# A two-layer trunk on one Trainium2 core: sixteen more weight tiles split into pairs ahead of their use, h put into PSUM by ScalarE for the output projection, and more time for two kinds of transfers

## The chip, the core and the metric

The kernel runs on one core of a Trainium2 chip. The core has a matmul engine (TensorE, PE in the profile, with its weight loads as PEld), three engines for everything else (VectorE, DVE; ScalarE, ACT; GpSimd, POOL), and a synchronising engine (SyncE, SP) that here issues nearly all transfers between the chip's memory and on-chip memory (SBUF), over 16 DMA engines. Matmuls write into PSUM, in eight banks of 128 x 512 float32. The engines run side by side and wait for each other by semaphores; each takes its own instructions in the order in which they stand. The metric is the device time of one execution, in microseconds, as the median of several runs.

## The reference

The reference is a decoder trunk on one sequence of 1024 tokens with 1024 features, in two layers, all in float32. Layer 0 mixes tokens with a gated MLP over chunks of 128 tokens, layer 1 with dilated windowed attention in three groups of heads, whose outputs are merged by their softmax weights. After each mixer comes a dense MLP of width 4096 with a squared ReLU:

```
x = x + mixer_i(rms_norm(x, g))                      i = 0: gating, 1: attention
x = x + relu(rms_norm(x, g') @ w_up[i]) ** 2 @ w_down[i]
...
out = rms_norm(x, g_final)

# attention, per dilation group: unnormalised sums, then merged
m_all = max over groups of m_;   c = exp(m_ - m_all)
o = sum(num * c) / sum(den * c);   x = x + o @ w_out
```

## The kernel before

Activations are kept transposed, features on partitions: `h[m]` is features 128m to 128m+127 by 1024 tokens, worked on in two halves of 512 tokens. A float32 operand is **split** into a pair: ScalarE writes a rounded high part (L213) and VectorE the remainder (L214). One product of two pairs is three matmuls, `three` at L326: high by high, high by low, low by high. All matmuls are issued at L185; six of them of 128 x 512 take about 1.36 us when TensorE does not wait.

The program runs through these stages (us from the start of the profiled execution): gating mixer to 305; first MLP, up to 623 and down to 910, closing to 936; values and attention to 1448; output projection to 1520; second MLP, up to 1823 and down to 2123; final norm to 2162.

**MLP.** The hidden width is worked on in 16 steps q. The first two are done plainly for the two halves of tokens; from q = 2 on, each step is a scheme of seven products (a, d, e and so on in `mlp`) of sums of weight tiles with sums of activations, 84 matmuls, about 19 us a step. `Weights` (L337) loads four raw tiles of a step, forms their sums on GpSimd and splits the seven results one by one, one at each call of `more`; each result goes into a slot that a product of the step before has freed. In layer 0, from q = 5 on, the second, fourth and sixth call of `more` also advance `prepare_late`, a side line that loads a weight tile of a later stage, splits it and stores the pair in memory (`wl`), where `late` fetches it ready for use. Before, it does this for eight tiles of the second MLP's first steps and eight of the output projection. The down phase (`Down`) does likewise seven products at a time over groups of up to four steps, adding into `h` in SBUF by VectorE (L962). The sums that several products share are kept in `u` (L981). Its last part, `close`, multiplies the hidden tiles of q = 15 (`xe`) by plain weights (`we`).

**Attention.** Twelve units of heads go through scores, softmax, transposes (`turned`) and values. The seven products of each unit's q, k weights come from `prepare`, which loads four raw tiles of a unit, waits a given time (`own is raw`: 8000 ns), then forms sums on VectorE (L487, L488 and on), splits them and stores them in memory (`wd`). `exchange` sends the softmax sums of a unit through memory into the order of another group; `merge` combines three groups, with 12000 ns (`LAT["ex"]`) planned for the exchange. `split_N` makes a merged output a pair, `outs[hp, i]` for head pair hp and token half i.

**Output projection.** `project(i, hps)` runs over the eight column blocks m; for each it sums the products of the head pairs `hps` in a bank and VectorE adds the bank to `h[m]` (L313). First the head pairs 0 to 2 of half 0, then of half 1 as filling between the last attention unit's work, then the last head pair of each half, after which the half's norm and y for the second MLP are made (`start_terms`).

**Order of the work.** TensorE's instructions stand in the order in which the program issues them (`manual_schedule` for TensorE). While it issues, `Flow` keeps a planned clock of TensorE's time, to which each matmul adds its length, and side lines (`flow.add`) whose steps are put in when the planned clock has reached their due time (`yield` of a time, or of an event and a time after it). `flow.until` moves the planned clock on until something is there. So the times in `LAT`, the `yield`s and the delay given to `flow.add` decide between which matmuls a side line's matmuls stand; nothing makes the real engines keep to them. The other engines' order comes from a scheduler. `bias_rows` (L1039) is such a side line: three times it loads a table, waits 12000 ns, casts it on ScalarE (L1045), multiplies it by the bias table and stores the row.

## Time and profile before

| | |
|---|---|
| median of 3 runs | 2161.12 us (2159.89 to 2166.99) |
| the profiled execution, its own time | 2163.61 us |
| its span in the trace | 2161.9 us |
| mean granted TensorE clock | 0.992 |
| matmul records | 10192 |
| DMA traffic | 367.68 MB, 170 GB/s on average |

The page gives busy time, share of the span and count for each engine. A group of instructions is named by line, engine, operation and tiles (`out<-in`, buffer numbers left out). Behind a row of the timeline stands in brackets how long the engine was idle before it, and what ended that. The numbers behind the engines in a row of windows are the granted TensorE clock, the share of the 16 DMA engines in use, and GB/s. TensorE's instructions are all L185 (matmuls) or L192 (transposes), so places in the program are told by tiles and time: `y` is a normalised input, `wp` a weight pair, `mm` and `at` are banks, `r` and `t` raw tiles and temporaries, `V` a unit's values, `o` a merged output.

### The profile page before, as it was taken

What the parts mean: (1) busy time and instruction counts of PE and PEld (TensorE: products, weight loads), DVE (VectorE), ACT (ScalarE), POOL (GpSimd) and SP (SyncE); (2) the same over time, 40 slices, a digit from 0 to 9 for tenths busy, and PEclk for the clock granted to TensorE, in tenths of its full rate; (3) what the DMA queues carried; (4) which work ended last, traced back from release to release, by engine and by line L of the source; (5) the groups of instructions that cost most, each with busy time, mean ns of one, the idle gap of its engine ahead of it and who ended that gap; (6) DMA issues with size and microseconds to landing.
All of it is one profiled execution on the core that took longest, in us unless ns stands there. A gap on an engine that the chain in (4) does not pass through costs nothing.

```text
span 2161.9 us, 30552 instructions
## 1 busy us (share of the span) xinstructions
PE 2119.5 (98%) x10192; PEld 1747.0 (81%) x10192; DVE 1560.9 (72%) x2897; ACT 1143.8 (53%) x2308; POOL 510.7 (24%) x381
## 2 busy tenths in 40 slices
PE   8999998999999999999999999999999999999997
PEld 7888887888888888878877788777788888888886
DVE  7877678655689787798357666758885555988776
ACT  7645445555565444355266665645455556544442
POOL 2000224323323333420200000001433322333344
PEclk9999999999999999999999999999999999999999
DMA  6326713566655443359787646491254443654432
GB/s 215 124 81 217 274 57 133 180 213 219 217 167 194 155 160 118 103 183 335 269 280 228 178 153 180 158 268 40 84 190 152 157 159 115 207 169 145 149 99 78
DMA packets 214962, 367.68 MB, mean 170 GB/s; under 512 B 38809, under 2 KB 66580, under 8 KB 214804
## 3 DMA queue, kind: packets, MB, share of 16 engines
q1 hardware_dynamic: 205664, 364.37, 50.5%
q10 hardware_dynamic: 9140, 1.36, 0.4%
q8 instruction: 80, 1.31, 0.2%
q14 instruction: 78, 0.64, 0.1%
HBM read 239.13 MB, written 126.52 MB: 169 GB/s over the span
## 4 chain that ended last, share of the span: by engine, by line
PE 81%; DVE 8%; DMA 4%; ACT 3%; issue 2%; SPq 0%; POOL 0%; DVEq 0%; POOLq 0%; ACTq 0%
PE at L185 42%; PE mm L185 39%; PE at L192 1%; DMA wp<-wd 1%; DVE h L313 1%; DVE hx L214 1%; DVE t L1486 1%; DVE tr L214 1%; DVE y L214 1%; DMA h<-in_xT 0%; DVE wp L214 0%; ACT t L1319 0%; DVE N L1358 0%; DMA r<-in_w_v 0%; DVE r L415 0%
## 5 line engine op out<-in xcount | busy, mean ns | idle before, releaser
L213 ACT ACTIVATE wp<-r 128x512 fp32r<-128x512 f32 (+2 forms) x411 | 243.8, 598 | 360.7 <-PE at L185 276.7
L214 DVE TENSOR_TENSOR wp<-r,wp 128x512 fp32r<-128x512 f32 (+2 forms) x404 | 323.7, 806 | 129.7 <-ACT wp L213 126.1
L185 PE MATMUL at<-hx,wp 128*128 128x512 f32 x1740 | 405.7, 389 | 1.4 <-DVE h L962 1.4
L185 PEld LDWEIGHTS at<-hx,wp 128*128 128x128 f32 x1740 | 326.5, 188 | 70.0 <-DVE h L962 2.2
L185 PE MATMUL mm<-t,wp 128*128 128x512 f32 x1368 | 345.5, 396 | 1.0 <-DVE k L1243 1.0
L185 PEld LDWEIGHTS mm<-t,wp 128*128 128x128 f32 x1368 | 251.2, 188 | 55.0 <-DVE k L1243 2.1
L269 POOL TENSOR_TENSOR t<-t 128x512 f32<-128x512 f32 (+1 forms) x64 | 81.9, 1281 | 714.6 <-ACT t L264 558.3
L185 PE MATMUL at<-y,wp 128*128 128x512 f32 x1008 | 246.5, 391 | 0.0
L185 PEld LDWEIGHTS at<-y,wp 128*128 128x128 f32 x1008 | 189.9, 189 | 40.2 <-issue 0.7
L185 PE MATMUL mm<-y,wp 128*128 128x512 f32 x816 | 216.5, 405 | 1.9 <-issue 1.2
L356 POOL TENSOR_TENSOR t<-r 128x512 f32<-128x512 f32 (+3 forms) x62 | 80.1, 1291 | 470.0 <-DMA r<-in_w_up 148.8
L185 PEld LDWEIGHTS mm<-y,wp 128*128 128x128 f32 x816 | 152.5, 193 | 35.2 <-issue 2.2
L185 PE MATMUL mm<-hx,wp 128*128 128x512 f32 x696 | 169.1, 389 | 0.0
L214 DVE TENSOR_TENSOR hx<-t,hx 128x512 fp32r<-128x512 f32 x192 | 156.7, 820 | 3.2 <-ACT hx L213 2.9
L185 PE MATMUL mm<-y,whi 128*128 128x512 f32 x512 | 158.1, 390 | 0.0
L185 PEld LDWEIGHTS mm<-hx,wp 128*128 128x128 f32 x696 | 130.4, 188 | 27.9 <-DVE b L981 0.9
L358 POOL TENSOR_TENSOR r<-r 128x512 f32<-128x512 f32 (+3 forms) x62 | 90.9, 1466 | 181.4 <-DVE wp L214 162.5
L213 ACT ACTIVATE hx<-t 128x512 fp32r<-128x512 f32 x192 | 119.6, 630 | 25.4 <-DMA t<-hid 20.0
L185 PE MATMUL at<-t,wp 128*128 128x512 f32 x552 | 130.6, 389 | 0.0
L962 DVE TENSOR_TENSOR h<-h,at 128x512 f32<-128x512 f32 x144 | 98.0, 681 | 42.6 <-PE at L185 42.0
L185 PEld LDWEIGHTS at<-t,wp 128*128 128x128 f32 x552 | 103.6, 188 | 21.5
L185 PEld LDWEIGHTS mm<-y,whi 128*128 128x128 f32 x512 | 95.6, 188 | 19.5
(225 smaller groups left out, 3452.8 us busy)
## 6 DMA issues: line engine op xcount, KB each, us to landing
t<-hid SPq DMA_DIRECT2D x182, 256.0 KB, 4.0
wd<-tr SPq DMA_DIRECT2D x154, 256.0 KB, 3.3
wp<-wd SPq DMA_DIRECT2D x77, 512.0 KB, 5.3
hid<-t SPq DMA_DIRECT2D x140, 256.0 KB, 2.9
r<-in_w_up SPq DMA_DIRECT2D x120, 256.0 KB, 2.7
r<-in_w_dn SPq DMA_DIRECT2D x80, 256.0 KB, 2.6
hid<-b SPq DMA_DIRECT2D x56, 256.0 KB, 2.9
r<-in_w_v SPq DMA_DIRECT2D x48, 256.0 KB, 3.7
```

The lines of the kernel that those rows point to most:

```text
L185: nc.tensor.matmul(out, lhsT, rhs, **kw)
L192: nc.tensor.transpose(out, src, ident)
L213: nc.scalar.activation(hi, src, AF.Copy)
L214: (engine or nc.vector).tensor_tensor(lo, src, hi.bitcast(F32), op=ALU.subtract)
L269: nc.gpsimd.tensor_tensor(self.acc, self.acc, sq, op=ALU.add)
L313: nc.vector.tensor_tensor(x, x, ps, op=ALU.add)
L356: tt(r3, r[0, 0], r[1, 0], op=ALU.subtract)
L358: tt(r[1, 1], r[1, 0], r[0, 0], op=ALU.subtract)
L962: return engine.tensor_tensor(hs[i, s], hs[i, s], src, op=ALU.add).ins
L1486: nc.vector.tensor_tensor(own(t, g), permuted(us_[g].N, i, g), own(pb, g), op=ALU.mult)
```

## The change

- `LATE` has 16 more tiles: the closing weights of both MLPs (`dl`) and the first set of value weights (`vt`). They are no longer split where they are used but loaded as pairs with `late`. The side line now does one tile at each of its turns: it loads the next tile and splits the one before, in place (the remainder is written over the raw tile). The two stores of a tile are issued at the next turn (`save`). So the steps q = 5 to 15 of layer 0 take three tiles each where they took one and a half. Each added tile costs two more stores of 256 KB in memory traffic and a load of 512 KB in place of one of 256 KB.
- In the down phase, from t = 4 on, the shared sum stays in PSUM: ScalarE copies the bank to a second bank (`sums`), and the product with w[6] is accumulated there, where VectorE added the bank to `u` before. 28 such adds of VectorE become 28 copies of ScalarE.
- In `project` for head pairs 0 to 2, ScalarE copies h into the bank before the products and the bank back into h after them. Only the column blocks 0 to 5 are done so; blocks 6 and 7 of each half are done at the end with all four head pairs in one bank, and added by VectorE.
- Planned times: the bias rows begin 120000 ns later, with 6000 ns between cast and matmul; raw weights get 18000 instead of 8000 ns; the exchange 15000 instead of 12000 ns, and a merge waits for both exchanges and 3000 ns.

`Weights` also gets a parameter for its order, whose default is the order as it was.

```diff
 OPEN = 5
+WHOLE = 6
+FIRST = 6
 LATER = (2, 4, 6)
 ...
 PACE = (2100.0, 2500.0, 1900.0, 3500.0)
-LAT = dict(sum=2600.0, rms=2600.0, tile=1600.0, gate=8500.0, soft=5500.0, turn=4200.0, fe=1300.0, v=2000.0, qk=4200.0, merge=2600.0, out=700.0, fex=3.0, ve=1600.0, vd=6000.0, ex=12000.0)
+LAT = dict(sum=2600.0, rms=2600.0, tile=1600.0, gate=8500.0, soft=5500.0, turn=4200.0, fe=1300.0, v=2000.0, qk=4200.0, merge=2600.0, out=700.0, fex=3.0, ve=1600.0, vd=6000.0, ex=15000.0)
 ...
             r00, r10, r01, r11 = (load(w_qkv[n + a][:, half(b)], own()) for a, b in ((0, 0), (1, 0), (0, 1), (1, 1)))
-            yield max(pace, 8000.0) if own is raw else pace
+            yield max(pace, 18000.0) if own is raw else pace
 ...
-    LATE = {("up", q, i, j): (w_up[1, q, i, j]) for q in range(2) for j in range(2) for i in range(2)}
+    LATE = {("dl", 0, a): w_dl[0, a] for a in range(4)}
+    LATE.update({("up", q, i, j): (w_up[1, q, i, j]) for q in range(2) for j in range(2) for i in range(2)})
     LATE.update({("bo", hp, b): w_bo[hp][:, half(b)] for hp in range(4) for b in range(2)})
+    LATE.update({("vt", k): w_vt[0, k] for k in range(KT)})
+    LATE.update({("dl", 1, a): w_dl[1, a] for a in range(4)})
     wl = {key: dram.tile([P, 2, HALF], F32, name="wl" + "_".join(map(str, key)), bufs=1) for key in LATE}
 ...
+    def fetch(src):
+        r = rtemp()
+        return r, load(src, r.bitcast(F32))
+
+    unsaved = []
+
+    def save():
+        for dst, t in unsaved:
+            nc.sync.dma_start(dst, t.bitcast(F32))
+        unsaved.clear()
+
+    def placed(dst, held):
+        lo, r = held
+        hi = rtemp()
+        split(hi, lo, r)
+        unsaved.extend((dst[:, e, :], t) for e, t in enumerate((hi, lo)))
+
 ...
-        for key, src in LATE.items():
-            r = load(src, temp())
+        keys = list(LATE)
+        held = fetch(LATE[keys[0]])
+        yield
+        for n, key in enumerate(keys):
+            last, held = held, fetch(LATE[keys[n + 1]]) if n + 1 < len(keys) else None
+            placed(wl[key], last)
             yield
-            hi, lo = rtemp(), rtemp()
-            split(hi, lo, r)
-            for e, t in enumerate((hi, lo)):
-                nc.sync.dma_start(wl[key][:, e, :], t.bitcast(F32))
-            yield
 ...
-    def late(*key):
-        t = wpool.tile([P, 2, HALF], F32R, tag="w", name="wp")
-        nc.sync.dma_start(t.bitcast(F32), wl[key])
-        return Pair(t)
+    def late(*key, place=None):
+        w = (place or wpair)()
+        nc.sync.dma_start(w.t.bitcast(F32), wl[key])
+        return w
 ...
                 if layer == 0 and q >= OPEN and calls[0] in LATER:
+                    save()
                     next(coming_late, None)
+                if layer == 0 and q == 15 and calls[0] == 7:
+                    save()
 ...
                     more()
-                    nc.vector.tensor_tensor(self.u[a], self.u[a], a_, op=ALU.add)
+                    sums = mm_bank()
+                    nc.scalar.activation(sums, a_, AF.Copy)
                     self.inputs(t + 1, (1,))
 ...
                     self.ends(1)
-                b = at_bank()
-                product(b, w[6], xs(6))
+                b = at_bank() if t < 4 else sums
+                product(b, w[6], xs(6), t >= 4)
                 then(nc.vector.tensor_tensor(self.u[a], self.u[a], b, op=ALU.add).ins, 6)
 ...
                 self.xe = {}
-                self.we = [pair("we").split(load(w_dl[self.layer, a], temp())) for a in range(4)]
+                self.we = [late("dl", self.layer, a, place=lambda: pair("we")) for a in range(4)]
             for j in range(2):
 ...
             nc.scalar.activation(oh[0:33, 0:VEC], raw[0:33, 0:VEC], AF.Copy)
+            yield 6000
             ps = at_bank()
 ...
     def value_weights(r, place=None):
+        if r == 0:
+            return [late("vt", k) for k in range(KT)]
         return [(place or wpair)().split(load(w_vt[r, k])) for k in range(KT)]
 ...
-    flow.add(bias_rows())
+    flow.add(bias_rows(), 120000.0)
     firsts = []
 ...
     ex = {}
+    exchanged = {(hp, g): Event() for hp in range(4) for g in (1, 2)}
 ...
         ex[u.hp, g] = e
+        exchanged[u.hp, g].t = flow.t
 ...
+        for g in (1, 2):
+            yield exchanged[hp, g], 3000
         us_ = {u.g: u for u in U if u.hp == hp}
 ...
-    def project(i, hps, after=None):
-        for m in range(KT):
-            b = mm_bank()
+    def project(i, hps, after=None, ms=range(KT)):
+        held, ms = {}, list(ms)
+
+        def begin(m):
+            held[m] = mm_bank()
+            if not after:
+                nc.scalar.activation(held[m], h[m][:, half(i)], AF.Copy)
+
+        begin(ms[0])
+        for n, m in enumerate(ms):
+            b = held.pop(m)
             for hp in hps:
-                three(b, wbo[hp, m // 4], blk(m % 4), outs[hp, i], hp == hps[0], hp == hps[-1])
+                three(b, wbo[hp, m // 4], blk(m % 4), outs[hp, i], bool(after) and hp == hps[0], hp == hps[-1],
+                      skip_group_check=True)
+                if hp == hps[0] and n + 1 < len(ms):
+                    begin(ms[n + 1])
                 flow.pump()
-            add_h(m, half(i), b)
             if after:
+                add_h(m, half(i), b)
                 after(m)
+            else:
+                nc.scalar.activation(h[m][:, half(i)], b, AF.Copy)
             yield
 ...
     flow.pump()
-    for _ in project(0, range(3)):
+    for _ in project(0, range(3), ms=range(FIRST)):
         pass
 ...
     outs_load(2, 1)
-    rest = project(1, range(3))
+    rest = project(1, range(3), ms=range(WHOLE))
     while (3, 0) not in outs and next(rest, 1) is None:
 ...
         proj_load(3, b)
-    for _ in project(0, [3], sq[0].add):
+    for _ in project(0, [3], sq[0].add, range(FIRST)):
         pass
+    if FIRST < KT:
+        for _ in project(0, range(4), sq[0].add, range(FIRST, KT)):
+            pass
     start_terms(sq[0], 0, 3, terms)
 ...
     flow.until(lambda: (3, 1) in outs)
-    for _ in project(1, [3], sq[1].add):
+    for _ in project(1, [3], sq[1].add, range(WHOLE)):
         pass
+    if WHOLE < KT:
+        for _ in project(1, range(4), sq[1].add, range(WHOLE, KT)):
+            pass
     start_terms(sq[1], 1, 3, terms)
 ...
         first[q][i, j] = late("up", q, i, j)
```

Three places of the new order matter for the steps of the prediction. Lines of the changed program are 3 to 31 higher than those of the profile of before; the lines named below are those that each program itself has.

TensorE, at the start of the second half's products in the opening of layer 0's MLP. Before; `tr,tab` are the two matmuls of a bias row, `y,wp` the MLP's:

```order
L185 MATMUL mm<-y,wp 128x512 x9
L185 MATMUL at<-tr,tab_3197 8x384
L185 MATMUL at<-tr,tab_3198 8x384
L185 MATMUL at<-y,wp 128x512 x3
L185 MATMUL mm<-y,wp 128x512 x9
```

After, where the first bias row now stands, in the middle of one of the seven products of a step of the up phase (`t` are sums of activations):

```order
L188 MATMUL mm<-t_3327,wp 128x512 x3
L188 MATMUL mm<-t_3364,wp 128x512 x3
L188 MATMUL at<-tr,tab_3213 8x384
L188 MATMUL at<-tr,tab_3214 8x384
L188 MATMUL mm<-t_3401,wp 128x512 x3
L188 MATMUL mm<-t_3438,wp 128x512 x3
L188 MATMUL at<-y,wp 128x512 x12
```

The other two rows moved likewise, each into a later step.

VectorE, at the first sum of the last unit's raw weights in attention (`r<-r`), with the splits of transposed probabilities (`tr<-at,tr`) and the score rows (`ISA`). Before:

```order
L1317 ISA t,st_10604<-at,b 128x128
L1317 ISA st_10604 128x1
L1358 TENSOR_TENSOR N<-N,at 64x256
L487 TENSOR_TENSOR r<-r 128x512
L1358 TENSOR_TENSOR N<-N,at 64x256
L214 TENSOR_TENSOR tr<-at,tr 128x256 x2
L1243 SCALAR_TENSOR_TENSOR q_10770<-mm,q_10769 128x512
```

After, two score sets later (the sum is L491 now):

```order
L1348 ISA st_10661 128x1
L1389 TENSOR_TENSOR N<-N,at 64x256
L1274 SCALAR_TENSOR_TENSOR k_10911<-t,k_10910 128x512
L1120 COPY b<-t 128x512
L491 TENSOR_TENSOR r<-r 128x512
L1279 TENSOR_TENSOR t<-t,mm 128x512
L1274 SCALAR_TENSOR_TENSOR q_10832<-t,q_10831 128x512
L1389 TENSOR_TENSOR N<-N,at 64x256 x2
L217 TENSOR_TENSOR tr<-at,tr 128x256 x2
```

The splits that stood right behind the sum now stand ahead of it; others stand behind it.

TensorE, from the sums of squares of the first half (`ones`) to the second MLP. Before:

```order
L185 MATMUL mm<-o,wp 128x512 x15
L185 MATMUL at<-ones,t 128x1 x12
L185 MATMUL mm<-o,wp 128x512 x15
L192 MATMUL at<-ident,rq 128x128 x4
L185 MATMUL mm<-o,wp 128x512 x48
L185 MATMUL mm<-y,wp 128x512 x9
```

After:

```order
L188 MATMUL mm<-o,wp 128x512 x45
L188 MATMUL at<-ones,t 128x1 x12
L188 MATMUL mm<-o,wp 128x512 x15
L195 MATMUL at<-ident,rq 128x128 x4
L188 MATMUL mm<-o,wp 128x512 x12
L188 MATMUL mm<-y,wp 128x512 x9
```

Of the projection's matmuls, 12 instead of 48 stand between the spread of the half's norm (`ident,rq`) and the MLP's first. Of all of them, 108 instead of 90 stand ahead of the first that takes the last head pair's output of half 0, and 42 instead of 78 between the end of half 0's projection and the MLP; the copies `mm<-h` and `h<-mm` of blocks 0 to 5 stand on ScalarE's queue between attention's exponentials and its casts.

More of the change, by code (lines that the diff above doesn't have):

```diff
@@ L337, in trunk, with __init__ @@
     class Weights:
-        def __init__(self, src, own=None, place=None):
-            self.own, self.place = own or raw, place or wpair
+        def __init__(self, src, own=None, place=None, order=(5, 6, 2, 7, 3)):
+            self.own, self.place, self.order = own or raw, place or wpair, order
             self.w = {}
@@ L362, in steps @@
             yield
-            for p, src in ((5, r[1, 0]), (6, r[1, 1]), (2, r[0, 1]), (7, r3), (3, r[0, 0])):
-                self.split(p, src)
+            src = {5: r[1, 0], 6: r[1, 1], 2: r[0, 1], 7: r3, 3: r[0, 0]}
+            for p in self.order:
+                self.split(p, src[p])
                 yield
@@ L928, in weights @@
                     runs.append([k, k + 1])
[L929 removed]
+            return Weights(lambda i, j: [w_dn[self.layer, a, i, j][:, lo * P:hi * P] for lo, hi in runs],
+                           **kw)
         def take(self, k, src, which):
```

2 lines of the change are left out of this document (1 added, 1 removed).

## The prediction

> **What bounds the kernel now.** I read the page first, then the groups of TensorE's waits, then the timeline and the windows around each wait that the change touches.
>
> ```profile
> span 2161.9 us, 30552 instructions
> PE 2119.5 (98%) x10192; PEld 1747.0 (81%) x10192; DVE 1560.9 (72%) x2897; ACT 1143.8 (53%) x2308; POOL 510.7 (24%) x381
> PE 81%; DVE 8%; DMA 4%; ACT 3%; issue 2%; SPq 0%; POOL 0%; DVEq 0%; POOLq 0%; ACTq 0%
> ```
>
> TensorE is busy for 2119.5 of 2161.9 us, and 81% of the chain that ended last is TensorE. The change has the same matmuls as before, so what can be won or lost is TensorE's idle time, 42.4 us by these two numbers, and the time that it runs at a lower clock. The waits by what ended them (total us, times, longest):
>
> ```profile
> PE at L185 <- ACT tr L1045: 6.3, 1, 6.3
> PE mm L185 <- DVE h L313: 4.2, 8, 1.5
> PE at L185 <- DMA V<-vd: 3.1, 1, 3.1
> PE at L185 <- issue: 1.3, 1, 1.3
> ```
>
> The first is the bias rows' cast, the second the adds of projections into h, the third the last attention unit's values, the fourth stands beside the raw weights of the last units (below). The change edits each of these places but the third.
>
> **The bias rows (moved by 120 us, 6 us between cast and matmul).** In the timeline (start, length, then engine, line, operation; a wait in brackets):
>
> ```profile
> 327.73 1.52 PE L185 MATMUL at<-y,wp 128*128 128x512 f32 x6
> 335.58 0.81 PE L185 MATMUL at<-tr,tab 33*8 33x384 f32 x2 [6.33 <-ACT tr L1045]
> 336.32 2.93 PE L185 MATMUL mm<-y,wp 128*128 128x512 f32 x6
> 339.04 2.57 PE L185 MATMUL at<-y,wp 128*128 128x512 f32 x6
> 342.84 1.52 PE L185 MATMUL at<-y,wp 128*128 128x512 f32 x6
> 344.20 1.52 PE L185 MATMUL mm<-y,wp 128*128 128x512 f32 x6
> 351.00 0.84 PE L185 MATMUL at<-y,wp 128*128 128x512 f32 x3
> 351.77 0.51 PE L185 MATMUL at<-tr,tab 33*8 33x384 f32 x2
> 335.02 0.51 ACT L1045 ACTIVATE tr<-t 33x384 fp32r<-33x384 f32 x1
> 330.45 2.36 DVE L214 TENSOR_TENSOR y<-r,y 128x512 fp32r<-128x512 f32 x2
> 336.00:341.00 5.00, 5.00 (x13) 3.72 (x12) 4.21 (x4) 0.76 (x2) 2.43 (x2) 0.50 0.07 23
> ```
>
> TensorE is in order: two small matmuls wait 6.33 us for a cast that ScalarE starts at 335.02, and the MLP's matmuls stand behind them. Then the granted clock is 0.50 (the number after the engines in the window row): three groups take 2.93, 2.57 and 0.81 us instead of 1.52, 1.52 and 0.51, which is 2.8 us more. In the new order the bias matmuls stand in three later steps of the up phase, each behind a cast issued 6 us earlier, so the most to gain is 6.33 + 2.8 = 9.1. What is late next is the MLP's own y: the last one split there is done at 330.45 + 2.36 = 332.81. If the very next matmul needed it, TensorE would still stand still from 327.73 + 1.52 = 329.25 to 332.81, which leaves 2.8 of gain. But ten groups of six matmuls stand between 336.32 and the use at 351.00, and six take 344.20 − 342.84 = 1.36 us, so without the wait that use comes at 329.25 + 13.6 = 342.9, 10 us after the split. I take 9.1 (bounds 2.8 and 9.1).
>
> **Raw weights of the last units (8 us to 18 us between load and use).**
>
> ```profile
> 1128.81 3.42 SPq L174 DMA_DIRECT2D r<-in_w_qkv  x2
> 1137.73 0.69 DVE L487 TENSOR_TENSOR r<-r 128x512 f32<-128x512 f32 x1 [6.58 <-DMA r<-in_w_qkv]
> 1138.91 0.76 DVE L214 TENSOR_TENSOR tr<-at,tr 128x256 fp32r<-128x256 f32 x2
> 1138.98 1.66 PE L185 MATMUL at<-tr,V 128*128 128x128 f32 x8 [1.29 <-issue]
> 1138.00:1144.00 6.00, 4.91 (x27) 4.16 (x28) 5.12 (x18) 3.47 (x13) 0.00 (x0) 0.67 0.58 219
> 1144.00:1160.00 16.00, 16.00 (x85) 13.16 (x84) 12.19 (x36) 9.12 (x28) 0.00 (x0) 0.91 0.87 210
> ```
>
> VectorE stands 6.58 us at the sum of raw weights, with the softmax splits (L214, tr) queued behind it; TensorE waits for those splits, 1.29 us, and the clock is then 0.67 for 6 us and 0.91 for 16: 6 × 0.33 + 16 × 0.09 = 3.4 us lost. In the new order the sum stands two score sets later, behind those splits, and its loads are planned 10 us more. Undone wholly that is 4.7. I take 3.5, since another wait may set the clock back in the same stretch (bounds 0 and 4.7).
>
> [...] The window row shows 0.67 right at a wait of 1.29, so I go by the row.
>
> **Exchanged sums given longer.** The merges' transposes move a few matmuls later between attention's; no long wait of before is theirs. The wait at the end of attention is for the values:
>
> ```profile
> 1423.00 3.73 SPq L1213 DMA_DIRECT2D V<-vd  x4
> 1433.42 1.84 PE L185 MATMUL at<-tr,V 128*128 128x128 f32 x8 [3.07 <-DMA V<-vd]
> 1430.00:1440.00 10.00, 6.93 (x32) 5.57 (x31) 3.07 (x7) 2.04 (x5) 0.00 (x0) 0.68 1.07 320
> 1440.00:1480.00 40.00, 40.00 (x249) 33.29 (x248) 27.90 (x101) 22.01 (x69) 0.00 (x0) 0.95 0.50 149
> ```
>
> The queue's order around those loads is as before, so I take 0. If the wait went, it would return 3.07 and the clock's 10 × 0.32 + 40 × 0.05 = 5.2, that is 8.3.
>
> **Value weights, and MLP closing weights, split in the up phase.** Before, eight value tiles are split while the first MLP closes:
>
> ```profile
> 922.39 1.82 DVE L214 TENSOR_TENSOR wp<-r,wp 128x512 fp32r<-128x512 f32 x1 [0.72 <-ACT wp L213]
> 924.86 2.35 PE L185 MATMUL mm<-xe,we 128*128 128x512 f32 x9 [1.51 <-DVE h L313]
> ```
>
> A split of 1.82 stands ahead of the add that empties the bank, and TensorE waits 1.51. The splits leave VectorE there, and I take the wait as gone: 1.5 (bounds 0 and 1.5). Their cost goes to the up phase, to 11 steps q = 5 to 15 that get three tiles each instead of one and a half:
>
> ```profile
> 530.00:587.00 57.00, 57.00 (x253) 47.19 (x253) 32.37 (x44) 33.69 (x59) 16.42 (x12) 1.00 0.62 212
> 528.45 2.88 PE L185 MATMUL at<-y,wp 128*128 128x512 f32 x12
> 532.52 0.69 DVE L214 TENSOR_TENSOR wp<-r,wp 128x512 fp32r<-128x512 f32 x1 [1.18 <-ACT wp L213]
> 547.49 1.75 PE L185 MATMUL at<-y,wp 128*128 128x512 f32 x7
> 701.00:758.00 57.00, 57.00 (x253) 47.18 (x253) 45.37 (x65) 26.49 (x42) 19.04 (x12) 1.00 0.48 155
> 550.41 0.58 ACT L862 ACTIVATE mm<-at 128x512 f32<-128x512 f32 x1 [0.56 <-PE at L185]
> ```
>
> Three steps (57 us) have VectorE busy 32.37 and ScalarE 33.69, and 4.5 more splits add about 4.5 × 0.69 = 3.1 to each. A weight whose slot the product at 528.45 frees is split by 532.52 + 0.69 and used at 547.49, 14 us later. So 4.5 more transfers a step on SP's queue, and the splits, cost 0; without that cover each us of delay is paid in 11 steps. Transfers did not stop TensorE at a share of 0.87 either (16.00 of 16 in the window from 1144). The down phase loses 28 of VectorE's adds and gets 28 ScalarE copies from PSUM to PSUM, of 0.58 each by the same shape at 550.41. The copy is read three products after it is made possible, so two stand between; a product of twelve matmuls covers 2.7 us; with no cover it would be 28 × 0.58 = 16. TensorE has no wait in the stage from 701 (57.00 of 57). I take 0 for both (bounds −1.4, were all waits for VectorE's adds to go, and +3).
>
> **Output projection.** h goes into the bank by ScalarE and comes out by ScalarE, for six of eight column blocks in each half: 24 copies × 0.58 = 14 us, and 12 of VectorE's adds fewer. Two blocks of each half wait for the last head pair, so less filling is left at the end: 42 matmuls (9.5 us) instead of 78 (17.7 us) between the first half's last block and the MLP.
>
> ```profile
> 1489.67 0.96 PE L185 MATMUL mm<-o,wp 128*128 128x512 f32 x3 [1.16 <-DVE h L313]
> 1520.66 0.94 PE L185 MATMUL mm<-y,wp 128*128 128x512 f32 x3 [1.16 <-issue]
> 1493.53 2.47 DVE L313 TENSOR_TENSOR h<-h,mm 128x512 f32<-128x512 f32 x4
> 1508.82 0.69 DVE L214 TENSOR_TENSOR y<-keep,y 128x512 fp32r<-128x512 f32 x1
> ```
>
> For: seven waits for adds, 4.2 − 1.5 = 2.7, and 1.16 at the MLP's start, 3.9 in all. Against: the copies stand among attention's exponentials, and from the last add of the first half (1496.0) to the first y (1509.5) went 13.5 us, against 9.5 and the norm's own few matmuls in between now: 1 to 4 us short, up to 6 with copies late. I take −1.0 (bounds −3.9 and +6), nearest to the waits' own rows, since ScalarE has 18 of 40 us free there.
>
> **Sum.** −9.1 − 3.5 − 1.5 − 1.0 = −15.1. The profiled execution took 2163.61 us by its own time, with a span of 2161.9; the median of the runs is 2161.12, so the sum against the span gives 2146.8, and against the median 2146.0. I forecast **2146**.
>
> **The rivals.**
> 1. *The value wait goes too* (the loads ahead of it shift): 2146.0 − 8.3 = 2138. For it: SP's queue carries other loads at other moments. Against: its order there is the same. 0.12.
> 2. *Some of the gain is not there*: the bias wait is replaced by one for y (+6.3), or the projection costs 5 instead of giving 1 (+6), or the raw wait stays, the change then not doing what it says (+3.5). One or two of them: 2151 to 2158. The order speaks against the first, nothing decisive against the second. 0.23.
> 3. *A wash*: all three, 2158 to 2166. 0.10.
> 4. *Slower: ScalarE's queue in the last attention unit.* The 24 copies stand in order ahead of exponentials and of p's casts; 12 of them wait for a TensorE product. If TensorE is then led by the softmax chain, each of 12 pairs costs two copies, 1.16, and about half of a nine-matmul product, 1.0: 26 us with nothing hidden, 2146.0 + 1.0 + 26 = 2173. It decides from the point at which ScalarE is full: 22.01 + 14 = 36 of 40 us in the window from 1440, near but below. [...] 0.10.
>
> **How the numbers follow.** The forecast (2141 to 2151) has 0.45. A difference of 0.3%, 6.5 us, is what a measurement here can tell from none: faster is below 2154.6. Faster holds the forecast, rival 1 and about half of rival 2: 0.69. Same holds the rest of 2 and rival 3: 0.21. Slower is rival 4: 0.10. The range 2137 to 2162 leaves out rival 4, the top of 3 and the foot of 1, about 0.2.
>
> **What would show it.** Right: no bias row among TensorE's waits, and a clock of 1.00 at 330 to 341; the raw sum (L491 after) without a wait of over 2 us for its load; no wait near 925; TensorE with no new wait from 1440 on in the middle of attention's last unit. The projection's step is wrong if TensorE waits for ScalarE's h or mm, or for y at the MLP's start, over 3 us; the up phase's if TensorE waits for wp between 370 and 620. The forecast is wrong as a whole if a new wait of over 8 us stands anywhere.

## The result, and the profile after

| | before | after |
|---|---|---|
| median of 6 runs | 2160.51 us (2156.78 to 2166.99) | 2145.66 us (2143.78 to 2154.69) |
| ratio | | 0.9933, 95% interval 0.9909 to 0.9956 |
| span of the profiled execution | 2161.9 us | 2144.5 us |
| TensorE idle in it (span less busy time) | 42.4 us | 32.9 us |
| DMA traffic | 367.68 MB | 384.47 MB |

The change makes the kernel 0.4% to 0.9% faster, about 15 us, and the forecast of 2146 is met. As will be seen, it is met in the sum and not in every term.

The DMA traffic is 16.8 MB higher, 1.05 MB for each of the sixteen tiles. So a tile adds two stores of 256 KB and a load of 512 KB; its raw load of 256 KB is not replaced, as the section on the change has it, but moves to the side line.

The page of the changed kernel, its first two lines and the chain by engine:

```profile
span 2144.5 us, 30686 instructions
PE 2111.6 (98%) x10192; PEld 1745.2 (81%) x10192; DVE 1537.3 (72%) x2853; ACT 1168.5 (54%) x2360; POOL 507.1 (24%) x381
PE 87%; DVE 5%; DMA 4%; ACT 3%; issue 2%; POOL 0%; SPq 0%; DVEq 0%; POOLq 0%; ACTq 0%
```

The matmuls are as many; TensorE is busy for 7.9 us less with them, and its share of the chain is 87% instead of 81%. Some 5 of the 7.9 are the lower clock: from 100 to 2100 us the clock is at one half for 27.3 us before and for 17.1 after, and I count half of that time as lost (at 1493 in the last section, 3.41 us at half the clock make fifteen matmuls 1.58 us longer). The rest was not followed. Of what TensorE still waits for in the changed kernel (total us, times, longest), these rows matter here:

```profile
PE mm L188 <- DVE k L1274: 6.0, 6, 2.6
PE at L188 <- DVE t L1521: 2.3, 1, 2.3
PE mm L188 <- ACT t L1284: 2.3, 1, 2.3
PE mm L188 <- DVE h L316: 0.7, 2, 0.4
```

The bias row's 6.3 and the values' 3.1 have gone from the head of this list, and the adds of the projections (L316 now) wait 0.7 instead of 4.2. New are three waits of 2.3 to 2.6 in attention, which no term of the prediction had; in a second execution of the same kernel they are 2.5, 1.1 and 2.1.

To place them, the start of the first matmul of each stage in both timelines, as lengths of stages (us):

| stage, from its first matmul to the next one's | before | after | difference |
|---|---|---|---|
| first MLP, opening and up phase | 322.50 | 314.22 | −8.28 |
| its down phase | 286.70 | 287.18 | +0.48 |
| its closing | 26.35 | 23.18 | −3.17 |
| value projections | 157.00 | 157.03 | 0 |
| attention, up to the output projection (at 1448.1 before, 1435.0 after) | 354.42 | 352.25 | −2.17 |
| output projection | 72.54 | 66.36 | −6.18 |
| second MLP, opening | 50.87 | 54.12 | +3.25 |
| all after it | 590.37 | 589.04 | −1.33 |

Place by place, in the changed kernel. First windows (us, busy time of the engines, then the granted clock, DMA share and GB/s):

```profile
326.00:341.00 15.00, 14.69 (x65) 12.17 (x66) 13.72 (x15) 8.70 (x17) 8.76 (x6) 1.00 0.38 141
1118.00:1126.00 8.00, 5.68 (x35) 4.44 (x35) 2.20 (x12) 4.01 (x14) 0.00 (x0) 0.99 0.90 264
530.00:587.00 57.00, 57.00 (x253) 47.22 (x252) 34.53 (x49) 36.20 (x63) 17.85 (x12) 1.00 0.77 272
1430.00:1470.00 40.00, 40.00 (x263) 33.78 (x262) 26.00 (x99) 33.32 (x92) 0.00 (x0) 1.00 0.49 165
1508.00:1515.00 7.00, 7.00 (x21) 5.65 (x21) 2.96 (x9) 0.78 (x2) 0.00 (x0) 0.51 0.00 0
```

Where the bias row stood (326 to 341) TensorE is busy 14.69 of 15 at a clock of 1.00: that wait has gone whole. The up phase (530 to 587) has its added splits and transfers, DMA share 0.77 instead of 0.62, and TensorE is still at 57.00 of 57. In the last unit (1430 to 1470) ScalarE is at 33.32 of 40 with the copies of h and TensorE at 40.00. And the clock is 0.51 at 1508 to 1515, at the second MLP's start, where it was 1.00 before.

Then attention's timeline around the raw weights, which is where the new waits are:

```profile
1118.30 2.30 SPq L177 DMA_DIRECT2D r<-in_w_qkv  x1
1120.69 4.20 SPq L488 DMA_DIRECT2D wd<-tr  x2
1123.86 0.69 DVE L217 TENSOR_TENSOR tr<-r,tr 128x512 fp32r<-128x512 f32 x1 [5.12 <-DMA wd<-tr]
1124.49 0.60 ACT L1284 ACTIVATE t<-mm 128x512 f32<-128x512 f32 x1 [3.77 <-DMA wd<-tr]
1125.14 4.60 PE L188 MATMUL mm<-t,wp 128*128 128x512 f32 x12 [2.32 <-ACT t L1284]
1125.43 0.45 SPq L177 DMA_DIRECT2D r<-in_w_qkv  x1
...
1129.87 1.04 SPq L488 DMA_DIRECT2D wd<-tr  x2
1130.97 0.46 SPq L177 DMA_DIRECT2D r<-in_w_qkv  x1
1131.52 0.89 SPq L488 DMA_DIRECT2D wd<-tr  x2
1132.45 0.49 SPq L177 DMA_DIRECT2D r<-in_w_qkv  x1
...
1138.56 0.69 DVE L491 TENSOR_TENSOR r<-r 128x512 f32<-128x512 f32 x1 [3.31 <-DMA r<-in_w_qkv]
1140.00 0.63 ACT L1273 ACTIVATE q<-t 128x512 fp32r<-128x512 f32 x1 [5.00 <-DVE t L1279]
1144.21 0.96 PE L188 MATMUL mm<-t,wp 128*128 128x512 f32 x3 [2.56 <-DVE k L1274]
...
1189.55 0.64 ACT L216 ACTIVATE tr<-r 128x512 fp32r<-128x512 f32 x1 [2.41 <-DMA wd<-tr]
1193.87 1.50 PE L188 MATMUL at<-k,q 64*128 64x128 f32 x11 [2.32 <-DVE t L1521]
```

Read it from the TensorE rows backwards. At 1125 TensorE waits for a copy of ScalarE, and ScalarE for a store of a prepared weight pair (`wd<-tr`), whose tile it needs; that store stands in the transfer queue among the raw loads of the next unit. At 1144 it waits for k, k stands behind the raw sum L491 on VectorE, and that sum still waits 3.31 us for its load. At 1194 a store is late again. (The buffers `t` and `tr` come from one pool, so a store that is late holds up whatever needs the next `t`.) So the raw weights' wait did not go: it became three.

### The profile page after: what moved, and what is told of

It reads as the page before. It is cut to its first block, busy times and chain, and to the rows that moved or that the text cites. A ratio compares the mean times of both kernels' runs of the same rounds, so it can differ in the third digit from the quotient of the medians.

```text
span 2144.5 us, 30686 instructions
## 1 busy us (share of the span) xinstructions
PE 2111.6 (98%) x10192; PEld 1745.2 (81%) x10192; DVE 1537.3 (72%) x2853; ACT 1168.5 (54%) x2360; POOL 507.1 (24%) x381
## 2 busy tenths in 40 slices
DMA packets 221875, 384.47 MB, mean 179 GB/s; under 512 B 39577, under 2 KB 67348, under 8 KB 221716
## 3 DMA queue, kind: packets, MB, share of 16 engines
q10 hardware_dynamic: 9140, 1.36, 0.5%
## 4 chain that ended last, share of the span: by engine, by line
PE 87%; DVE 5%; DMA 4%; ACT 3%; issue 2%; POOL 0%; SPq 0%; DVEq 0%; POOLq 0%; ACTq 0%
PE mm L188 45%; PE at L188 41%; PE at L195 2%; DMA wd<-tr 1%; DMA od<-o 1%; DMA h<-in_xT 1%; DVE tr L217 0%; DMA r<-in_w_v 0%; DVE t L1678 0%; DMA V<-vd 0%; ACT t L1350 0%; ACT k L1273 0%; DVE y L217 0%; DVE k L1274 0%; DMA o<-od 0%
## 5 line engine op out<-in xcount | busy, mean ns | idle before, releaser
L216 ACT ACTIVATE wp<-r 128x512 fp32r<-128x512 f32 (+3 forms) x403 | 238.4, 597 | 345.4 <-PE at L188 213.1
L217 DVE TENSOR_TENSOR wp<-r,wp 128x512 fp32r<-128x512 f32 (+3 forms) x396 | 312.6, 794 | 147.6 <-ACT wp L216 144.6
L188 PE MATMUL mm<-t,wp 128*128 128x512 f32 x1368 | 347.9, 397 | 8.3 <-DVE k L1274 6.0
L188 PE MATMUL at<-hx,wp 128*128 128x512 f32 x1452 | 340.6, 389 | 0.6 <-DVE h L989 0.6
L188 PEld LDWEIGHTS at<-hx,wp 128*128 128x128 f32 x1452 | 272.4, 188 | 57.9 <-DVE h L989 1.1
L188 PE MATMUL mm<-hx,wp 128*128 128x512 f32 x984 | 234.4, 389 | 1.0 <-DVE hx L217 1.0
L188 PEld LDWEIGHTS mm<-hx,wp 128*128 128x128 f32 x984 | 184.6, 188 | 39.7 <-DVE hx L217 1.3
L217 DVE TENSOR_TENSOR hx<-t,hx 128x512 fp32r<-128x512 f32 x192 | 164.4, 862 | 8.8 <-ACT hx L216 8.7
```

Source lines behind the costliest of these rows:

```text
L188: nc.tensor.matmul(out, lhsT, rhs, **kw)
L216: nc.scalar.activation(hi, src, AF.Copy)
L217: (engine or nc.vector).tensor_tensor(lo, src, hi.bitcast(F32), op=ALU.subtract)
```

## The experiments

Each kernel is the changed one with one edit, except where it is said; "attention" is the stage of the table above (before 354.4, after 352.3). Ratios are to the kernel before, run beside them.

| run | median us | ratio (95%) | attention | other stage that answers |
|---|---|---|---|---|
| bias undone | 2156.92 | 0.9976 (0.9962 to 0.9989) | 354.2 | opening and up 322.2 |
| raw 8000 | 2137.74 | 0.9899 (0.9872 to 0.9926) | 345.2 | |
| exchange undone | 2158.87 | 0.9983 (0.9973 to 0.9994) | 358.3 | projection 71.6 |
| projection undone | 2151.37 | 0.9949 (0.9931 to 0.9966) | 354.8 | projection 71.0, opening 50.2 |
| late tiles undone | 2149.16 | 0.9943 (0.9922 to 0.9963) | 352.1 | closing 25.8 |
| down sums undone | 2146.00 | 0.9928 (0.9912 to 0.9943) | 357.6 | down 287.9 and 286.8 |
| raw 18000 for the last unit alone | 2137.90 | 0.9887 (0.9871 to 0.9903) | 347.2 | |
| before, with the exchange's change | 2154.31 | 0.9962 (0.9947 to 0.9977) | 347.0 | projection 69.5 |
| the changed kernel again | 2146.15 | 0.9923 (0.9906 to 0.9939) | 354.7 | |
| raw 8000 again | 2139.66 | 0.9897 (0.9879 to 0.9914) | 347.9 | |
| raw 3500 | 2137.47 | 0.9882 (0.9862 to 0.9902) | 347.4 | |
| raw 8000, exchange 18000 | 2143.45 | 0.9910 (0.9894 to 0.9926) | 349.3 | projection 68.4 |

**Bias rows undone.**

```diff
-            yield 6000
...
-    flow.add(bias_rows(), 120000.0)
+    flow.add(bias_rows())
```

> The changed kernel with the bias rows as before: begun at once, no time between cast and matmul. Theory (the bias wait and the slow clock behind it were worth what the opening and up phase got shorter, 322.50 to 314.22 us in the two traces): the wait of about 6.3 us at a bias row's cast comes back, the clock is 0.5 for about 6.8 us behind it, and the time is 8.3 us above the changed kernel, about 2154. Rival (the splitting of fewer tiles in place and the rest of the change carry part of it): under 5 us above.

Its timeline:

```profile
335.24 0.80 PE L188 MATMUL at<-tr,tab 33*8 33x384 f32 x2 [6.34 <-ACT tr L1073]
```

And its window there:

```profile
332.00:341.00 9.00, 5.76 (x16) 4.07 (x17) 7.77 (x8) 3.19 (x6) 4.82 (x3) 0.62 0.31 95
```

The wait and the low clock are back at the same place, and opening and up phase take 322.2 instead of 314.2 us: 8 us, as the theory has it. The median is 11 us up; the 3 us beyond that are in attention and later, where one kernel's executions differ by as much (the attention of the changed kernel itself: 352.3 and 354.7).

**Raw weights at 8000 ns.**

```diff
-            yield max(pace, 18000.0) if own is raw else pace
+            yield max(pace, 8000.0) if own is raw else pace
```

> The changed kernel with 8000 ns instead of 18000 ns between load and use of the last units' raw weights. TensorE stands in the same order; VectorE, ScalarE and the transfer queue do not. In the changed kernel the stretch from the first scores to the first unit's transposes got 4.2 us longer than before, where I had forecast 3.5 less. Theory (the longer time is the cause: the next raw loads and the stores behind them stand so that VectorE and ScalarE wait for stored tiles and for the raw load, and TensorE for them): the waits of 2.3, 2.6 and 2.3 us at 1125, 1144 and 1194 go, the stretch is 3 to 5 us shorter, about 2141 in all. Rival (the merges' later steps are the cause): these three waits stay within 1 us, time 2146.

The same stretch of its timeline, transfer queue, VectorE and TensorE:

```profile
1113.25 1.22 SPq L177 DMA_DIRECT2D r<-in_w_qkv  x2
1117.09 3.49 SPq L177 DMA_DIRECT2D r<-in_w_qkv  x2
1125.93 0.69 DVE L491 TENSOR_TENSOR r<-r 128x512 f32<-128x512 f32 x1 [6.50 <-DMA r<-in_w_qkv]
1127.18 1.41 PE L188 MATMUL at<-tr,V 128*128 128x128 f32 x8 [1.23 <-issue]
```

And its window there:

```profile
1120.00:1150.00 30.00, 28.40 (x164) 22.37 (x163) 18.34 (x55) 15.86 (x50) 0.00 (x0) 0.94 0.81 266
```

The raw loads go out at 1113 to 1120 instead of 1118 to 1132, VectorE waits 6.50 us for them as it did before the change, TensorE once for 1.23 us, and none of the three new waits is there. Attention takes 345.2 us, 7.1 less. That is the theory, which gave 3 to 5 for a stretch of the stage. Of this, 5.6 us are TensorE's idle time in the stage (12.8 to 7.2 us), and the rest is mostly clock; when both kernels were run once more (below), the idle time fell by 5.8 (13.4 to 7.6). By its median this kernel is faster than both the kernel before and the changed one.

**Exchange and merges undone.**

```diff
-LAT = dict(..., ex=15000.0)
+LAT = dict(..., ex=12000.0)
...
-        for g in (1, 2):
-            yield exchanged[hp, g], 3000
```

> The changed kernel with the exchange planned at 12000 ns and merges that do not wait for it, as before. In the changed kernel the wait for the last unit's values went from 3.07 to 0.14 us, with the slow clock behind it, some 6.4 us, though I had forecast no change there. Theory (TensorE stands in another order around it, since the merges' transposes come later): the wait is back at about 3 us, the last stretch of attention 5 to 6 us longer; from the merges themselves no other loss. Rival (it went because the first units' weights come at other moments, by the raw weights' longer time): the wait stays under 0.5 us. Second rival, to e2: the three new waits at 1125, 1144 and 1194 come from the merges and go here.

In its timeline the wait for the values, and at the projection's end one for the norm of the first half:

```profile
1426.51 1.94 PE L188 MATMUL at<-tr,V 128*128 128x128 f32 x8 [2.25 <-DMA V<-vd]
...
1505.43 0.62 PE L195 MATMUL at<-ident,rq 128*128 128x128 f32 x4 [2.54 <-DVE rq L255]
```

The first is back, and attention is 6 us longer; the projection is 5.3 us longer too, which the theory had not. Two of the three waits at 1125 to 1194 stay (1.9 and 2.6), and two of 2.6 and 2.7 for other operands stand in place of the third, so the second rival falls. The whole costs more than the theory's 5 to 6: 13 us by the medians.

**The output projection undone** (all blocks in two goes, added by VectorE: the function as before, `WHOLE` and `FIRST` 8).

> The changed kernel with the output projection as before: all eight blocks of each half in two goes, all added by VectorE. Theory (the projection's stretch got 6.2 us shorter and the second MLP's opening 2.6 us longer by it): the waits for adds of 0.2 to 1.2 us come back, the clock stays at 1.0 behind the second half's sums of squares, net 2 to 4 us above the changed kernel, 2148 to 2150. Rival (the shorter stretch comes from what stands ahead of it, so that the adds no longer collide): no change, 2146. Second rival (the copies cost in attention's last unit what the projection gains): some us below.

Its timeline at the end of the projection:

```profile
1487.82 3.70 PE L188 MATMUL mm<-o,wp 128*128 128x512 f32 x15 [0.99 <-DVE h L316]
1509.01 0.92 PE L188 MATMUL mm<-y,wp 128*128 128x512 f32 x3 [1.16 <-issue]
```

The waits for adds and the one at the MLP's start are back: 2.0 and 1.2 us, where the changed kernel waits 0.7 for adds. Projection and opening take 121.2 us together; in the nine profiled executions that have the new projection and the exchange at 15000 ns they take 115.7 to 120.5, on average 118.1, which by itself is too near to tell. But up to 5.1 us of these are lost to the half clock, which comes in some executions and not in others. Without that loss (half of the time at half clock) they take 119.5 with the old projection (119.8 in the kernel before with the exchange's change alone, below), and 115.3 to 116.8 with the new, on average 115.9. So the new one is worth about 3.6 us, and the first rival falls. The longer opening of the second MLP, of which the theory speaks, belongs to the clock and not to the projection: other executions with the new projection have 50.9 us there. The median, 5.7 us up, has attention's spread in it again.

**The sixteen tiles split where they are used.**

```diff
-    LATE = {("dl", 0, a): w_dl[0, a] for a in range(4)}
...
-    LATE.update({("vt", k): w_vt[0, k] for k in range(KT)})
-    LATE.update({("dl", 1, a): w_dl[1, a] for a in range(4)})
...
-                self.we = [late("dl", self.layer, a, place=lambda: pair("we")) for a in range(4)]
+                self.we = [pair("we").split(load(w_dl[self.layer, a], temp())) for a in range(4)]
...
-        if r == 0:
-            return [late("vt", k) for k in range(KT)]
```

> The changed kernel with the sixteen added tiles (closing weights and first value weights) split where they are used again; the side line keeps its new form for the other sixteen. Theory (their splits stood ahead of the adds that free the banks in the first MLP's closing, and the splits cost nothing in the up phase): the closing stage goes from 23.2 back to 26.3 us, the up phases and the down phases stay within 0.7 us, 3 us above the changed kernel, 2148 to 2149. Rival (more splits and transfers cost the up phase something): the stretch up to the down phase gets 1 us or more shorter, and the total is the same or less.

The closing stage in its timeline, where TensorE waits for the last sum of squares (L276); VectorE's adds into h, from which the squares are made, stand between splits again:

```profile
919.45 1.05 PE L188 MATMUL at<-ones,t 128*128 128x1 f32 x8 [1.66 <-DVE t L276]
```

It takes 25.8 us, 2.6 more than in the changed kernel, and the opening and up phase take 314.2, the same to 0.1 us with 16 tiles as with 32. The added work of the up phase costs nothing.

**The down phase's sums on VectorE again.**

```diff
-                    sums = mm_bank()
-                    nc.scalar.activation(sums, a_, AF.Copy)
+                    nc.vector.tensor_tensor(self.u[a], self.u[a], a_, op=ALU.add)
...
-                b = at_bank() if t < 4 else sums
-                product(b, w[6], xs(6), t >= 4)
+                b = at_bank()
+                product(b, w[6], xs(6))
```

> The changed kernel with the down phase's shared sums added by VectorE in SBUF again, 28 adds in place of 28 copies. Theory (both lie beside TensorE's work): the down phases, 287.2 and 286.5 us, stay within 0.6 us, and so does the time, 2145 to 2147. Rival (VectorE's free time there is worth something): the down phases together 1.5 us or more longer. Second rival (the copy delays the product that is added to it): together 1 us or more shorter.

The down phases take 1.0 us more together and the median is the same. The first was 287.2 to 288.4 us in executions of kernels that do not differ there, so this is no difference that can be told.

**18000 ns for the last unit alone.** The raw weights of two units are prepared in this way, one after the other; the wait is 18000 for the second and 8000 for the first.

```diff
-            yield max(pace, 18000.0) if own is raw else pace
+            yield max(pace, 18000.0 if i == 11 else 8000.0) if own is raw else pace
```

> The changed kernel with 18000 ns between load and use for the very last unit's raw weights alone, 8000 ns for the unit before it. With 8000 ns for both, attention up to the projection took 345.2 us, with 18000 ns for both 352.2. Theory (the longer time of the first of the two moves its sums and stores later, in between the raw loads of the second, which then wait, as do the stores' tiles): the raw loads go out at about 1113 to 1120 as with 8000 for both, VectorE waits for none of them, and the 345.2 us become some 343 to 344.5, about 2135 in all. Rival (what costs is the place of the last unit's sums among its scores, whoever's load is late): 350 us or more, as with 18000 for both.

Attention takes 347.2 us, so the rival falls: it is the first unit's 18000 that costs, since it moves that unit's stores into the second's loads. The theory is wrong in its other half. VectorE waited for that load at L491 here too, 6.80 us, and TensorE behind it for 1.5 us: planning more time for the last unit took none of the wait away. The raw loads go out at 1113 to 1121, as with 8000 for both.

**The kernel before, with the exchange's change alone.**

```diff
-LAT = dict(..., ex=12000.0)
+LAT = dict(..., ex=15000.0)
...
+        for g in (1, 2):
+            yield exchanged[hp, g], 3000
```

> The kernel before with the change to exchange and merges alone (15000 ns planned, merges wait for both exchanges and 3000 ns). Undoing it in the changed kernel brought the wait for the last unit's values back (2.3 us, clock 0.5 for 10 us) and cost 6 us in attention. Theory (it acts through the order of TensorE's instructions alone and needs none of the rest): the wait of 3.07 us at 1433 goes below 1 us, attention up to the projection gets 4 to 7 us shorter than 354.4, about 2155. Rival (it needs the longer time of the raw weights): the wait stays at 2 us or more, time within 2 us of the kernel before.

The values' wait in its timeline:

```profile
1431.58 1.08 PE L185 MATMUL at<-tr,V 128*128 128x128 f32 x8 [1.10 <-DMA V<-vd]
```

And its window there:

```profile
1426.00:1446.00 20.00, 18.90 (x115) 15.55 (x114) 9.70 (x32) 8.39 (x29) 0.00 (x0) 1.00 1.09 328
```

The wait is 1.10 instead of 3.07, just over the bound that the theory set, and the clock stays at 1.00 where it was 0.68; attention is 7.5 us shorter, and the median is 8.1 us under that of the kernel before. It needs nothing of the rest of the change. At this place 2.0 us are the wait and 5.1 the clock, which was at half for 10.2 us before; TensorE's idle time in the whole stage falls by only 1.5 us (10.8 to 9.3). That it acts through TensorE's order alone, as the theory says, is not shown: the loads of the values go out in the same order, but at 1421.62 instead of 1423.00.

**The changed kernel and 8000 ns again, 3500 ns, and a later exchange**, on one chip.

> The changed kernel as it is, beside the next three on one chip. Both theories: its ratio to the kernel before as measured first, 0.991 to 0.996.

> The changed kernel with 8000 ns for both units' raw weights, once more, to be set against the changed kernel on the same chip. Theory (the longer time costs 7 us in attention): ratio 0.987 to 0.992, 6 to 10 us under the changed kernel. Rival (the first comparison owed part to its chip): under 4 us.

> The changed kernel with 3500 ns, the steps' own pace, between load and use of the raw weights. Theory (the sooner the first unit's stores are out, the less they meet the second's loads; the wait of 6.5 us on VectorE for those loads stays): attention up to the projection within 1.5 us of the 345.2 us with 8000. Rival (planned sooner, the sums stand ahead of more of the scores' work, and VectorE waits longer for the loads): 348 us or more.

> The changed kernel with 8000 ns for the raw weights and the exchange planned at 18000 instead of 15000 ns. Theory (the later the merges stand, the later TensorE comes to the last unit's values; 0.55 us of that wait are left with 8000): the wait goes, up to 0.5 us in attention, nothing else, within 1.5 us of the kernel with 8000 and 15000. Rival (still later merges leave too little filling at the end of the projection): a wait of 1 us or more for the last merged outputs or for y, 2 us or more slower.

The changed kernel's ratio is 0.9923, within what was expected. With 8000 ns the median is 6.5 us under its. 3500 ns is as good as 8000: attention 347.4 against 345.2 and 347.9 in two executions. That is more than the 1.5 us of the theory from one of them and near the rival's 348, but VectorE waits no longer for the last unit's loads, as the rival needs: 5.3 us, against 6.5 and 7.1 with 8000. A later exchange takes nothing off: its median is 3.8 us above that of 8000 and 15000 ns on the same chip. In it the merged outputs are late for the projection, as the rival has it, and the values' wait is 2.88:

```profile
1421.69 1.08 PE L188 MATMUL at<-tr,V 128*128 128x128 f32 x8 [2.88 <-DMA V<-vd]
1475.64 0.49 PE L188 MATMUL mm<-o,wp 128*128 128x512 f32 x1 [1.86 <-ACT o L216]
```

The second execution of the changed kernel has the values' wait at 1.97 us, where the first had 0.14, and the order is the same:

```profile
1428.02 1.76 PE L188 MATMUL at<-tr,V 128*128 128x128 f32 x8 [1.97 <-DMA V<-vd]
```

So that wait is a race between a transfer and TensorE, which came out 1.8 us apart in two executions of one program, and a difference of 2 us in it, in one execution each, says nothing on a kernel. What the exchange's change does to attention stands on more runs: with 8000 ns or less for the first of the two units, 354.4 us without it (before, one execution) and 345.2 to 347.9 with it (five runs, each of another kernel or chip); with 18000 ns, 358.3 without it (one) and 352.1 to 357.6 with it (six runs, mean 354.3).

## Why the prediction was right, and where it was not

| term | predicted us (bounds) | shown |
|---|---|---|
| bias rows | −9.1 (−9.1 to −2.8) | −8 |
| raw weights | −3.5 (−4.7 to 0) | +7 |
| exchange and values' wait | 0 (−8.3 to 0) | −7.5 |
| tiles split early | −1.5 (−1.5 to 0) | −2.6 to −3.2 |
| down phase's sums | 0 (−1.4 to +3) | 0 |
| projection | −1.0 (−3.9 to +6) | −3.6 |
| sum | −15.1 | about −15 |

The terms shown come from single profiled executions and can be off by some microseconds, so that their sum is so near the measured −14.9 proves little. By the medians the raw weights cost 6.5 and 7.9, and the exchange is worth 8 in the kernel before and 13 in the changed one.

- **Bias rows: right, in mechanism and size.** The wait went whole and the next y was not late, as the count of matmuls up to its use said.
- **Raw weights: wrong, with the wrong sign.** The step that failed is "the sum stands two score sets later, behind those splits, and its loads are planned 10 us more". The last unit's loads are issued behind the first unit's steps, so the longer time of the first put them later too. It moved the first unit's stores with its steps, and the second unit's loads into the midst of those stores; the load was no more ahead of the sum than before. By the prediction's own sign, no wait of over 2 us at L491, the step failed: 3.31 us (1.94 in the second execution). And the splits that stood behind the sum only gave their place to the q and k of another unit, for which TensorE waits as well. The bound of "0" at the losing end was taken from the wait's own row and left out what the moved stores hold up. The stores of a moved step, and the queue that they go through, should have been followed as its sums were.
- **Exchange and values' wait: wrong in size.** "The queue's order around those loads is as before, so I take 0" looked at the transfer queue alone. TensorE's own order had changed too, and with it the moment at which it comes to the values. Which of the two moved the wait is not separated; that this change alone does it, and takes the clock's loss with it, is shown. The rival that named it had a chance of 0.12 and about the right price, 8.3.
- **Tiles split early: right in mechanism, the size a little small.** One wait was counted (1.51). A second of 0.48 ahead of the squares went with it, and stops too short to be listed: for the same 110 matmuls TensorE is busy for 24.3 us before and 23.2 after. Together that is 3.2 us in the two profiled executions, 2.6 by the run that undoes it. That the up phase hides the work is shown: 314.2 us with and without.
- **Down phase: right.** No difference that can be told.
- **Projection: right in sign, the size near the low bound.** Undone, it costs about 3.6 without the clock's loss. The shorter cover at the end, 42 matmuls instead of 78, did not make TensorE wait for the y of the second MLP; its one wait there is 0.44 us, for an add that frees a bank. The slower rival, ScalarE's queue in the last unit, did not happen: ScalarE at 33.32 of 40 us with TensorE at 40.00. (That an instruction there stands behind one that waits, the rival's condition, is seen in the changed kernel: a copy of N whose semaphore was last updated at 1178.56 starts at 1180.72, behind an activation that had waited 3.09 us, up to 1180.07.)

That the forecast is so near is luck: two terms of attention that were wrong by some 10 and 7.5 us have opposite signs, and the smaller misses of the other terms make up the rest. The kernel that has only the right ones, 8000 ns with the rest of the change, runs at 0.990 of the kernel before (0.9872 to 0.9926, and 0.9879 to 0.9914 again).

The low clock beside the raw weights' wait, 0.67 at a wait of 1.29 us in the prediction's window row, is there with 8000 ns too: a wait of 1.23 us has a mean clock of 0.94 around it (1120 to 1150), and twelve matmuls from 1130.17 on take 4.60 us, where twelve from 1122.94 on took 3.01. Between that wait and them TensorE worked for 3.0 us, on transposes and narrow matmuls. So the wait is not shown to be all of the low clock's cause.

Left open: why the projection got 5 us longer when the exchange's change was undone in the changed kernel. In that trace TensorE waits 4.7 us there, 2.5 for the norm, 1.5 for two adds into h and 0.7 for a copy of h by ScalarE, where the changed kernel has no wait in the stage. Why these came late was not followed.

## What to carry to other kernels

A planned time that stands between a load and its use moves all that comes after the use too, its stores and the next loads; before it is made longer, the stores that move with it and the buffers that they hold have to be followed through the queue. A forecast that fits should be taken apart by undoing each part of the change: here it hid a loss of 7 us that one number takes back. Where executions of one kernel differ by a clock that falls in some and not in others (here 5.29 and 3.71 us for the same fifteen matmuls), stages are compared by their waits and without that loss. Splitting weights ahead of time, in a stage whose vector engines have room, was free to within 0.1 us here.

## What the runs showed of the hardware

In each of the two traces, of before and of the changed kernel, the times between 100 and 2100 us at which the record of the granted clock falls to one half are a multiple of 3.413 us apart: 334.44, 1139.98, 1433.53 and 1501.80 us before are 236, 86 and 20 steps, 1125.80, 1194.06, 1494.43 and 1508.09 in the changed kernel 20, 88 and 4. In these two traces the steps at half the clock, thirteen of them, follow steps in which TensorE streamed few columns, idle or not. With 512 columns in 227 ns as full (six such matmuls take 1.36 us), and a matmul counted in the step in which it starts, each of the thirteen stood behind a step filled to 0.48 or less; a full clock followed none filled to less than 0.40, and between 0.40 and 0.48 both occurred. The step with the wait of 1.29 us among transposes and narrow matmuls was filled to 0.37 (ahead of 1139.98 before), and half the clock followed; behind the wait of 2.56 us at 1144 in the changed kernel, whose two steps were filled to 0.60 and 0.47, the clock stayed at 1.00. The sums of squares, 24 matmuls of one column in the trace, take about 2.7 us: TensorE is never idle from 1491.02 to 1494.43 in the changed kernel, a step filled to 0.40. In the changed kernel half the clock follows each of them, in the timeline at 1490.46 and 1505.87; the row by itself is the same place in its second execution:

```profile
1490.46 2.73 PE L188 MATMUL at<-ones,t 128*128 128x1 f32 x24
1493.06 5.29 PE L188 MATMUL mm<-o,wp 128*128 128x512 f32 x15
1505.87 3.08 PE L188 MATMUL at<-ones,t 128*128 128x1 f32 x24
```

```profile
1497.66 3.71 PE L188 MATMUL mm<-o,wp 128*128 128x512 f32 x15
```

The fifteen matmuls behind the first sums take 5.29 us there and 3.71 in the second execution, where the clock is 1.00 from 1498 to 1504: 1.58 us between two executions of one kernel at this place. The second MLP's opening took 54.1 us in this trace, 6.8 of them at half the clock, and 50.9 with 8000 ns. That it depends on where the sums lie in the steps of 3.413 us would fit these rows, but was not shown.
